# First unit of a decoder block without the shift of 256 features, its share added to the sums as a bias

## The chip, the core and the metric

The kernel runs on one core of one Trainium2 chip. A core has a matrix engine (TensorE, PE in the profile, with PEld for its weight loads), a vector engine (VectorE, DVE), an activation engine (ScalarE, ACT), a general engine (GpSimd, POOL) and a queue engine (SyncE, SP) that here issues every DMA. Each engine takes its instructions in order and waits on semaphores; the program fixes the order on each engine beforehand. The metric is the device time of one execution in microseconds (us); lower is better.

## The reference, cut to what matters

One layer, one sequence of 1024 tokens with 1024 features, all float32. The change touches only the first lines of the layer:

```python
mod = (cond @ w_ada[l] + b_ada[l])              # cond = silu(c), one vector of 1024
sh_a, sc_a, gt_a, sh_m, sc_m, gt_m = split(mod, 6)
h = rms_norm(x, g_attn_pre[l]) * (1 + sc_a) + sh_a
proj = h @ w_in[l]                              # 2304 columns: q, k, v of two mixers
...                                             # two attentions, w_out, gated residual
y = square(relu(h2 @ w_up[l])) @ w_down[l]      # the channel half, gated residual
```

Write `xn` for x divided by its root mean square. Then h = xn * g + s, with a scale g = g_attn_pre * (1 + sc_a) and a shift s = sh_a for each feature. A product with h is a product with xn * g, plus the row s @ w_in, which is the same for every token.

## The kernel before, in words

Every float32 product is done as three products of halves: each operand is split in a part rounded to the engine's fast type ("hi") and the rest ("lo"), and hi*hi, hi of the activations * lo of the weights (lines L920, L921) and lo of the activations * hi of the weights (L923) are added in one PSUM bank. `hw` holds hi and lo of h, transposed: feature chunk k (128 features, k = 0 to 7) by token.

The program is written out by a planner of the kernel's own (`Sched`), which runs when the program is built. Every piece of work is an operation with a booked duration, its dependences, the buffers it takes and gives (`Res`), and a priority; several operations may go to one of two engines, and the planner picks the one that ends earlier by its own figures. TensorE's work stands in streams ("xt" for transposes of x, "mod", "dense" for projections, "s", "t", "pv" for attention), and `prefer()` says which goes first: dense work is preferred as long as the projections lead the attention by less than `LEAD`, counted in units. What comes out is a fixed order on each engine.

**Loading.** SP issues, in the order of the list `order0`: the eight blocks of x (128 tokens each), the columns of `w_ada` for the shift and the scale of h (group g has the 256 features of chunks 2g and 2g+1; four tiles (g, j) of 512 KB, each with shift and scale columns side by side), and the six weight tiles of the first unit, ("w", i). `NWA` and `r_stg` are the buffers these go to, `WS` those of the raw weights, `WR` those of the split weights.

**Preparing.** For each block of x: ACT squares and sums it (L629), POOL adds epsilon and raises to -1/2 (L468, L470), ACT or DVE multiplies the block by that (L634, L635), TensorE transposes it in eight pieces (L642), ACT or DVE copies the result out of PSUM to `xnT` (L646). For each group: DVE multiplies eight 128x512 pieces of `w_ada` by `cond` and adds them up (L664, L666), TensorE sums over partitions (L675), and DVE makes g and s (L681 to L683). Then for each chunk: ACT writes hi (L705), ACT writes the full value in place (L702), DVE subtracts to get lo (L708). Group 0 does this in two halves of 512 tokens, the others at once.

**The first unit** (`first_unit`). A unit is a set of 384 columns of `w_in`: three column sets c by two token halves x, six PSUM banks, each summing eight chunks. There are six units. In the first, the six banks are filled side by side as the chunks become ready: chunks 0 and 1 for the first half, then for the second, then chunks 2 and 3 for both, 4 and 5, and at the end 6 and 7 bank by bank. While TensorE has nothing to do, `filler` puts in products of ones that nobody reads (L937) up to the first product of that bank. `evac` takes each finished bank out (on DVE the rotary embedding, L817 to L820; on ACT and DVE hi and lo). The next units use `proj_tile`: 24 products in a row in one of the two "pj" banks, after each other.

Attention, the output projection and the channel half follow. The code that is touched:

Of the kernel before, what the change touches and what calls it, by code (L numbers as in the profile page):

```python
# [177 lines left out]
class Sched:  # L178
# [57 lines left out]
    def spare(self, o):  # L236

        return self.slack if 15 <= o.prio < 25 else 2.5 if o.kind == "w" else 0.0
# [24 lines left out]
    def pick(self, e):  # L263
        best = None
        q = self.queue[e]
        for o in q:
# [9 lines left out]
            key = (s + PW * o.prio if e != "SP" else s, o.prio, o.seq)  # L276
# [81 lines left out]
def hybrid_block(ctx: ExitStack, tc: tile.TileContext, x, positions, w_ada, b_ada, g_attn_post, w_in, w_out,  # L358
# [33 lines left out]
    WR, WS, NP, NV, NK, NQ, NT, NO = 6, 2, 4, 3, 2, 2, 2, 2  # L392
# [89 lines left out]
    order0 = [("x", 0), ("x", 1), ("x", 2), (0, 0), (0, 1), ("x", 3), (0, 2), ("w", 0), (0, 3), ("w", 1)]  # L482
    order0 += [("x", t) for t in range(4, TB)]
    for g in range(1, 4):
        order0 += [(g, 0), (g, 1), (g, 2), (g, 3)] + [("w", 2), ("w", 3), ("w", 4), ("w", 5)][(0, 0, 1, 3)[g]:(0, 1, 3, 4)[g]]
# [30 lines left out]
    def load_ada(g, j):  # L516

        def emit():
            wa_t[g, j] = stage("wa") if (g, j) in beside else place0("wa")
            for n in range(2):  # L520
# [26 lines left out]
    def split_w(*a):  # L547
# [10 lines left out]
        if a[0] == 0:  # L558
            w_e[a] = op("DVE", t_dv(512), lo(V), [e], gives=[(r_wst, 1)], prio=3)
        else:  # L560
            w_e[a] = op(("DVE", "POOL"), (t_dv(512), t_ptt(512)), (lo(V), lo(G)), [e], gives=[(r_wst, 1)], prio=3)
# [21 lines left out]
    e = op("ACT", 0.1, lambda: A.activation(cond[:], c_raw, AF.Exp, scale=-1.0), [e_c], prio=0)  # L583
# [6 lines left out]
    warm = p0.tile([P, KC], F32, name="warm")  # L590
# [35 lines left out]
    def x_block(tb):  # L626
        def f_sq():
# [24 lines left out]

    def mod_group(g):

        b = {}
# [30 lines left out]
        for half in ((0, 1) if g == 0 else (None,)):  # L686
# [6 lines left out]
    def mod_chunk(k, eg, half):  # L693
# [6 lines left out]
        def full(eng):  # L700
            if eng is A:
                return lambda: A.activation(h, h, AF.Identity, bias=s_a[:, k:k + 1], scale=g_a[:, k:k + 1])  # L702
            return lambda: V.tensor_scalar(h, h, g_a[:, k:k + 1], s_a[:, k:k + 1], ALU.mult, ALU.add)

        eh = op("ACT", t_sb(n) + 2 * AP_COST, lambda: A.activation(hh, h, AF.Identity, bias=s_a[:, k:k + 1],  # L705
                                                                  scale=g_a[:, k:k + 1]), deps, prio=0)
        e = op("ACT", t_sb(n) + 2 * AP_COST, full(A), [eh], prio=0)
# [21 lines left out]
    e_turned = op("POOL", 1.8, f_turned, [e_rope] + e_rs, prio=0)  # L729
# [241 lines left out]
    for a in first_unit():  # L971
        evac(*a)
# [1270 lines left out]
```

## Time and profile before

| | before |
|---|---|
| time, median of 3 runs | 1117.04 us (1116.61 to 1117.36) |
| the profiled execution | 1117.15 us, its span 1114.9 us (2.25 us lie around the span) |
| granted clock of TensorE | 0.998 |
| TensorE busy | 1100.7 us, 5393 products |
| VectorE, ScalarE, GpSimd busy | 819.5, 630.3, 247.9 us |
| first product of the first unit (L920) | 23.16 us |
| the second half of chunk 0 begins | 34.70 us |
| first product of the second unit (`pj`, L920) | 66.87 us |

"Busy" of TensorE counts matmuls whose ends are modelled and overlap, so the distance from start to start is what to read, not the length. An order of start times on one engine is a timeline; a row with xN merges N equal instructions, and the brackets tell what ended an idle time before it. A view by windows adds up each engine's busy time in a stretch.

### The profile page before, as it was taken

The page shows a single profiled execution, that of the slowest core. Times are in us where ns is not written, and L with a number is a line of the kernel's source. Part 1 is how long each engine was busy: PE and PEld are TensorE (multiplying, and loading weights), DVE is VectorE, ACT ScalarE, POOL GpSimd, SP SyncE. Part 2 cuts the span into 40 slices and gives each one's busy share as a digit, 9 for nine tenths or more (in the row PEclk, how much of TensorE's full clock was granted, in tenths as well). Part 3 has the DMA queues.
Part 4 walks back from the last instruction along what each step waited for, and adds up shares of the span by engine and source line. Part 5 has one row for each costly group of instructions (what it writes and reads, how often), then busy time and mean ns, then how long its engine had stood idle before and what let it go on. Part 6 is the DMA issues. An engine that isn't in the chain of part 4 may idle for free.

```text
span 1114.9 us, 15568 instructions
## 1 busy us (share of the span) xinstructions
PE 1100.7 (99%) x5393; PEld 917.0 (82%) x5393; DVE 819.5 (74%) x1388; ACT 630.3 (57%) x1092; POOL 247.9 (22%) x316
## 2 busy tenths in 40 slices
PE   8999999999999999999999999999999999999996
PEld 7788888888888888888888888888888888888885
DVE  7877777666777666689798654798643996537998
ACT  8768776464656666577674335643154632347542
POOL 2158768666742231110000000000000000000003
PEclk9999999999999999999999999999999999999999
DMA  9756676454513734656751369521578013584104
GB/s 350 227 180 192 195 261 198 146 207 159 186 43 140 263 103 131 227 211 243 276 217 38 109 240 334 175 76 39 201 267 308 26 57 113 189 320 152 39 20 151
DMA packets 94110, 195.39 MB, mean 175 GB/s; under 512 B 9008, under 2 KB 31664, under 8 KB 94032
## 3 DMA queue, kind: packets, MB, share of 16 engines
q1 hardware_dynamic: 94032, 194.40, 50.3%
q8 instruction: 43, 0.70, 0.3%
q14 instruction: 35, 0.29, 0.1%
HBM read 141.80 MB, written 33.03 MB: 157 GB/s over the span
## 4 chain that ended last, share of the span: by engine, by line
PE 85%; DVE 7%; DMA 3%; issue 2%; ACT 1%; SPq 0%; POOL 0%; POOLq 0%; DVEq 0%; ACTq 0%
PE mlp_ps L2057 17%; PE mlp_ps L2055 17%; PE mlp_ps L2056 17%; PE pj L920 5%; PE pj L923 5%; PE pj L921 4%; PE s_ps L1203 3%; PE y_ps L1609 2%; PE y_ps L1611 2%; PE y_ps L1610 2%; PE o_ps L1338 2%; DMA wa<-in_w_ada 2%; PE pt_ps L1308 1%; PE s_ps L1258 1%; PE o_ps L1350 1%
## 5 line engine op out<-in xcount | busy, mean ns | idle before, releaser
L2055 PE MATMUL mlp_ps<-hw 128*128 128x512 f32 x896 | 348.9, 389 | 0.2 <-DVE u L2092 0.2
L2057 PE MATMUL mlp_ps<-hw 128*128 128x512 f32 x896 | 348.6, 389 | 0.0
L2056 PE MATMUL mlp_ps<-hw 128*128 128x512 f32 x896 | 348.6, 389 | 0.0
L2055 PEld LDWEIGHTS mlp_ps<-hw 128*128 128x128 f32 x896 | 168.2, 188 | 35.5 <-DVE u L2092 0.6
L2056 PEld LDWEIGHTS mlp_ps<-hw 128*128 128x128 f32 x896 | 168.2, 188 | 35.1
L2057 PEld LDWEIGHTS mlp_ps<-hw 128*128 128x128 f32 x896 | 168.2, 188 | 34.7
L1819 DVE TENSOR_TENSOR hw<-w,hw 128x1024 fp32r<-128x1024 f32 x96 | 114.6, 1221 | 98.1 <-ACT hw L1812 97.9
L1812 ACT CAST hw<-w 128x1024 fp32r<-128x1024 f32 x96 | 97.7, 1048 | 127.5 <-PE mlp_ps L2057 86.8
L2165 POOL TENSOR_TENSOR st<-st,nhalf 128x1 f32<-128x1 f32 x8 | 8.0, 1010 | 591.8 <-DVE st L2163 591.8
L920 PE MATMUL pj<-hw,w_hl 128*128 128x512 f32 x240 | 102.3, 426 | 0.0
L923 PE MATMUL pj<-hw,w_hl 128*128 128x512 f32 x240 | 94.6, 394 | 0.0
L921 PE MATMUL pj<-hw,w_hl 128*128 128x512 f32 x240 | 94.3, 393 | 0.0
L1326 DVE TENSOR_TENSOR ph<-pt_ps,ph 128x512 fp32r<-128x512 f32 (+1 forms) x110 | 69.1, 647 | 31.4 <-ACT ph L1322 31.0
L1812 ACT CAST hw<-u 128x1024 fp32r<-128x1024 f32 x48 | 48.6, 1051 | 63.2 <-PE mlp_ps L2057 63.2
L1322 ACT CAST ph<-pt_ps 128x512 fp32r<-128x512 f32 (+1 forms) x110 | 58.4, 556 | 31.5 <-PE pt_ps L1311 25.2
L1819 DVE TENSOR_TENSOR hw<-u,hw 128x1024 fp32r<-128x1024 f32 x48 | 56.9, 1218 | 17.8 <-ACT hw L1812 17.8
L1229 ACT ACTIVATE p_sb<-p_sb,mn 128x128 f32<-128x128 f32 (+3 forms) x64 | 49.7, 777 | 33.6 <-DVE mn L1222 32.9
L1234 POOL TENSOR_SCALAR p_sb<-p_sb,den 128x128 f32<-128x128 f32 (+3 forms) x64 | 49.8, 783 | 75.6 <-DVE den L1232 69.6
L2113 DVE TENSOR_TENSOR yacc<-yacc,mlp_ps 128x512 f32<-128x512 f32 x96 | 62.0, 681 | 3.3 <-PE mlp_ps L2057 3.3
L1070 POOL TENSOR_TENSOR ada_acc<-ada_acc,wa_st 128x512 f32<-128x512 f32 x42 | 55.6, 1323 | 3.5
L923 PEld LDWEIGHTS pj<-hw,w_hl 128*128 128x128 f32 x240 | 45.1, 188 | 10.4
L1609 PE MATMUL y_ps<-hw,oh 128*128 128x512 f32 x128 | 52.1, 407 | 0.0
(215 smaller groups left out, 1971.0 us busy)
## 6 DMA issues: line engine op xcount, KB each, us to landing
hw<-s_dram SPq DMA_DIRECT2D x84, 512.0 KB, 4.3
wa_st<-in_w_ada SPq DMA_DIRECT2D x32, 512.0 KB, 5.2
w<-in_w_up SPq DMA_DIRECT2D x32, 512.0 KB, 5.6
w<-in_w_down SPq DMA_DIRECT2D x32, 512.0 KB, 6.7
s_dram<-hw SPq DMA_DIRECT2D x28, 512.0 KB, 3.8
qt<-hl SPq DMA_DIRECT2D x40, 256.0 KB, 2.6
w_st<-in_w_in SPq DMA_DIRECT2D x36, 256.0 KB, 3.0
x_sb<-in_x SPq DMA_DIRECT2D x16, 512.0 KB, 5.5
```

The costliest lines, as they stand in the source:

```text
L920: T.matmul(ps, w[:, 0, n], h[0], start=(k == 0), stop=False)
L921: T.matmul(ps, w[:, 1, n], h[0], start=False, stop=False)
L923: T.matmul(ps, w[:, 0, n], h[1], start=False, stop=(k == KC - 1))
L1322: A.copy(b["ph"][:, 0, :w], b["pt"][:, :w])
L1326: V.tensor_tensor(b["ph"][:, 1, :w], b["pt"][:, :w], b["ph"][:, 0, :w].bitcast(F32), ALU.subtract)
L1609: T.matmul(ps[:], b["oh"][:, k], wh[:, c0:c0 + 512], start=(k == 4 * m), stop=False)
L1812: A.copy(out[j][0], flat(src[j]))
L1819: V.tensor_tensor(out[j][1], flat(src[j]), out[j][0].bitcast(F32), ALU.subtract)
L2055: T.matmul(ps[m][:], sh, mh, start=starts and k == 0, stop=False, **kw)
L2056: T.matmul(ps[m][:], sh, ml_, start=False, stop=False, **kw)
L2057: T.matmul(ps[m][:], sl, mh, start=False, stop=k == 3, **kw)
L2113: e = op("DVE", t_dv(512), lambda: V.tensor_tensor(y(), y(), ps[m][:], ALU.add), [e, ml.e_y[tb, n]], gives=gives, prio=1)
```

## The change

The numbers of lines below are of the changed kernel where they are above L978 or so named.

- **Group 0** (`LATE = (0,)`): its four tiles of `w_ada` are cut the other way: two tiles hold scale columns alone, two hold shift columns alone. The two with the scale are loaded early, the two with the shift (named (10, 0), (10, 1)) last of all. `late_sums` sums either, with 128x256 pieces.
- **Chunks 0 and 1** of h are first made without the shift: ACT writes hi of xn*g, and one DVE instruction (`scalar_tensor_tensor`) writes lo from xnT, g and hi. The full value is not written.
- **The bias**: once s of these 256 features is there, twelve small products (`pb`, 128x2) multiply it with the first unit's weights, DVE adds hi and lo, and ACT adds the outcome to each of the six finished banks (`shift`) before `evac`. The weight tiles 0 to 2 stay until then.
- **Again**: after that, `mod_chunk(..., again=True)` makes chunks 0 and 1 with the shift (ACT hi, DVE full value, DVE lo, 1024 tokens at once) for the units that follow; their products wait for `e_rest`.
- **GpSimd** multiplies all eight blocks of x by their norm, and five of the full values of chunks 2 to 7 go to it.
- **Order and tables**: `order0` is another list; three buffers for raw weights instead of two; priorities weigh 0.03 us each in the first unit; weight loads are held back 1.5 us instead of 2.5; no filler stands by itself in front of a product of the first unit; `LEAD` is 1.0 instead of 0.8; the activation table for Exp is loaded by an instruction that waits for no DMA.

```diff
-        return self.slack if 15 <= o.prio < 25 else 2.5 if o.kind == "w" else 0.0
+        return self.slack if 15 <= o.prio < 25 else 1.5 if o.kind == "w" else 0.0
...
-    WR, WS, NP, NV, NK, NQ, NT, NO = 6, 2, 4, 3, 2, 2, 2, 2
+    WR, WS, NP, NV, NK, NQ, NT, NO = 6, 3, 4, 3, 2, 2, 2, 2
...
+    LATE = (0,)
+    order0 = [('x', 0), ('x', 1), ('x', 2), ('w', 0), ('x', 3), (0, 0), (0, 1), ('w', 1), ('x', 4), ('x', 5), (1, 0), ('x', 6), ('x', 7), (1, 1), (1, 2), ('w', 2), (1, 3), (2, 0), (2, 1), (2, 2), (2, 3), ('w', 3), (3, 0), ('w', 4), (3, 1), ('w', 5), (3, 2), (3, 3), (10, 0), (10, 1)]
...
-        e = op(("ACT", "DVE"), (t_sb(D) + AP_COST, t_d2(D) + AP_DV),
-               (lambda: A.mul(x_t[tb][:], x_t[tb][:], rstd[:, tb:tb + 1]),
-                lambda: V.tensor_scalar(x_t[tb][:], x_t[tb][:], rstd[:, tb:tb + 1], None, ALU.mult)), [e], prio=2)
+        e = op("POOL", t_pts(D),
+               lambda: G.tensor_scalar(x_t[tb][:], x_t[tb][:], rstd[:, tb:tb + 1], 1.0, ALU.mult, ALU.mult), [e], prio=1)
...
+        if k // 2 in LATE and not again:
+            eh = op("ACT", t_sb(n) + AP_COST, lambda: A.mul(hh, h, g_a[:, k:k + 1]), deps, prio=0)
+            e = op("DVE", t_dv(n) + AP_DV, lambda: V.scalar_tensor_tensor(
+                hl, h, g_a[:, k:k + 1], hh.bitcast(F32), ALU.mult, ALU.subtract), [eh], prio=0)
...
+        if again:
+            eh = op("ACT", t_sb(n) + 2 * AP_COST, lambda: A.activation(hh, h, AF.Identity, bias=s_a[:, k:k + 1],
+                                                                      scale=g_a[:, k:k + 1]), [eg] + e_used[k], prio=6)
+            e = op(("ACT", "DVE"), (t_sb(n) + 2 * AP_COST, t_d2(n) + 2 * AP_DV), (full(A), full(V)), [eh], prio=4)
+            e_rest[k] = op("DVE", t_dv(n), lambda: V.tensor_tensor(hl, h, hh.bitcast(F32), ALU.subtract), [e], prio=4)
+            return
...
-        e = op("ACT", t_sb(n) + 2 * AP_COST, full(A), [eh], prio=0)
+        e = op(("ACT", "POOL"), (t_sb(n) + 2 * AP_COST, t_pts(n) + 0.6), (full(A), full(G)), [eh], prio=0)
...
-        n = int(max(0.75 * idle, 0.5 * min(o.dur, 2.0)) / 0.22)
+        n = int(max(0.75 * idle, 0.0 if o.dur in (0.454, 0.227) else 0.5 * min(o.dur, 2.0)) / 0.22)
...
+                if LATE:
+                    def shift(a=a, c=c):
+                        A.activation(accs[a][:], accs[a][:], AF.Identity, bias=bias0[:, c:c + 1])
+                    d = op("ACT", t_ps(512) + AP_COST, shift, [d, e_bias], prio=2)
...
+            for c in range(3):
+                for k, part in jobs:
+                    i, n = w_at(0, c, k)
+                    T.matmul(b_ps[0][:, c], w_hl[0, i][:, part, n * P:n * P + P], s_hl[:, k],
+                             start=(k, part) == jobs[0], stop=(k, part) == jobs[-1])
...
-    LEAD = 0.8
+    LEAD = 1.0
```

How the instructions stand is shown at three places. The first is TensorE from the fourth block of x (`pxt` are its transposes, `pm` the sums of group 0, `acc<-ones_r` filler, `acc<-hw,w_hl` the first unit). Before:

```order
L642 MATMUL pxt<-head,x_sb 128x128 x8
L937 MATMUL acc<-ones_r 128x512 x3
L675 MATMUL pm<-ones,acc_a 128x1 x4
L937 MATMUL acc<-ones_r 128x512 x6
L642 MATMUL pxt<-head,x_sb 128x128 x8
L937 MATMUL acc<-ones_r 128x512
L920 MATMUL acc<-hw,w_hl 128x512
L921 MATMUL acc<-hw,w_hl 128x512
L937 MATMUL acc<-ones_r 128x512
```

and with the change:

```order
L644 MATMUL pxt<-head,x_sb 128x128 x8
L995 MATMUL acc<-ones_r 128x512
L673 MATMUL pm<-ones,acc_a 128x1 x2
L995 MATMUL acc<-ones_r 128x512 x7
L978 MATMUL acc<-hw,w_hl 128x512
L979 MATMUL acc<-hw,w_hl 128x512
L644 MATMUL pxt<-head,x_sb 128x128 x8
L978 MATMUL acc<-hw,w_hl 128x512
L979 MATMUL acc<-hw,w_hl 128x512
```

The transposes of the fifth block have moved behind the first product, two of four sums of group 0 are gone from here, and filler no longer stands between the products.

The second place is GpSimd, from its first instruction on x (`rs_t`, `rstd` are the two steps of the norm). With the change:

```order
L468 TENSOR_SCALAR rs_t<-ssq 128x1
L470 TENSOR_TENSOR rstd<-rs_t,nhalf 128x1
L637 TENSOR_SCALAR x_sb<-x_sb,rstd 128x1024
L468 TENSOR_SCALAR rs_t<-ssq 128x1
L470 TENSOR_TENSOR rstd<-rs_t,nhalf 128x1
L468 TENSOR_SCALAR rs_t<-ssq 128x1
L637 TENSOR_SCALAR x_sb<-x_sb,rstd 128x1024
L470 TENSOR_TENSOR rstd<-rs_t,nhalf 128x1
L637 TENSOR_SCALAR x_sb<-x_sb,rstd 128x1024
```

Before, the pairs L468, L470 follow each other with no scaling between them. The rows are of the second, third and fourth block: the scaling of the third stands behind the first step of the fourth.

The third place is GpSimd behind its last step on x, up to the low parts of weights that the second unit needs (`turned`, `tab` are the tables of the rotary embedding, `w_hl` the split weights, `hl` the first bank's result). Before:

```order
L725 COPY turned<-cosw 128x8x8 x2
L726 COPY turned<-sinw 128x8x16
L728 TENSOR_SCALAR turned<-turned 128x8x16 x2
L733 COPY tab_150<-head 128x1024
L734 MEMSET tab_151 128x1024
L555 TENSOR_TENSOR w_hl<-w_st,w_hl 128x512 x2
L826 TENSOR_TENSOR hl<-hl 128x512
L555 TENSOR_TENSOR w_hl<-w_st,w_hl 128x512 x2
L1249 COPY p_sb<-nsink 128x4 x2
```

and with the change:

```order
L783 COPY turned<-cosw 128x8x8 x2
L784 COPY turned<-sinw 128x8x16
L786 TENSOR_SCALAR turned<-turned 128x8x16 x2
L791 COPY tab_150<-head 128x1024
L792 MEMSET tab_151 128x1024
L748 TENSOR_SCALAR xnT<-xnT,g_a,s_a 128x1024 x2
L557 TENSOR_TENSOR w_hl<-w_st,w_hl 128x512 x2
L748 TENSOR_SCALAR xnT<-xnT,g_a,s_a 128x1024 x3
L557 TENSOR_TENSOR w_hl<-w_st,w_hl 128x512 x4
L884 TENSOR_TENSOR hl<-hl 128x512 x2
L557 TENSOR_TENSOR w_hl<-w_st,w_hl 128x512
```

Five full values (L748) are new, two behind the tables and three behind two weight tiles; and six weight tiles (L557) stand ahead of the first bank's low part (L884, L826 before) instead of two.

On TensorE the products after the first unit are the same in number; from the 2633rd before the end on they also stand in the same order, in the middle of the attention they are woven in another way. `pb` adds twelve, and there are 45 fillers instead of 61.

More of the change, by code (lines that the diff above doesn't have):

```diff
@@ L558, in split_w @@
         if a[0] == 0:
-            w_e[a] = op("DVE", t_dv(512), lo(V), [e], gives=[(r_wst, 1)], prio=3)
+            w_e[a] = op(("DVE", "POOL"), (t_dv(512), t_ptt(512) + 1.5), (lo(V), lo(G)), [e], gives=[(r_wst, 1)], prio=3)
         else:
@@ L582, in hybrid_block @@
     e_init = op("DVE", 0.4, f_init, prio=0)
-    e = op("ACT", 0.1, lambda: A.activation(cond[:], c_raw, AF.Exp, scale=-1.0), [e_c], prio=0)
+    warm = p0.tile([P, KC], F32, name="warm")
+    e = op("ACT", 1.5, lambda: A.activation(warm[:], nhalf[:], AF.Exp), [e_init], prio=0)
+    e = op("ACT", 0.1, lambda: A.activation(cond[:], c_raw, AF.Exp, scale=-1.0), [e_c, e], prio=0)
     def f_cond():
@@ L964, in after @@
                     sc.filler = None
+                if last[w] == i:
+                    w_used(w)
             d = dense(0.454 if part == 0 else 0.227, emit,
                       [w_e[0, w_at(0, c, k)[0]], (e_hl if part else e_hh)[k, x]] + (e_xn[0] + e_xn[1] if a == 5 else []),
-                      takes=[(r, 1)] if first else [], after=after, gives=[(r_w, 1)] if last[w_at(0, c, k)[0]] == i else [])
+                      takes=[(r, 1)] if first else [], after=after)
+            if c == 2 and part:
+                e_used.setdefault(k, []).append(d)
```

101 lines of the change are left out of this document (87 added, 14 removed).

## The prediction

> **What bounds the kernel now.** I read the page first, then TensorE's waits from 66 us on, then its order in time over the start, then VectorE's and GpSimd's.
>
> ```profile
> PE 1100.7 (99%) x5393; PEld 917.0 (82%) x5393; DVE 819.5 (74%) x1388; ACT 630.3 (57%) x1092; POOL 247.9 (22%) x316
> ...
> PE pm_o L1581 <- DVE o_sb L1575: 0.4, 1, 0.4
> ```
>
> TensorE is busy for 99% of the span, and from 66 us to the end it waits five times, 0.4 us at the most; the longest is shown. So whatever moves its work before 66 us moves the end by as much, unless a new wait appears later. The start:
>
> ```profile
> 23.16 0.39 PE L920 MATMUL acc<-hw,w_hl 128*128 128x512 f32 x1
> ...
> 34.70 0.39 PE L920 MATMUL acc<-hw,w_hl 128*128 128x512 f32 x1
> ...
> 42.62 0.95 PE L675 MATMUL pm<-ones,acc_a 128*128 128x1 f32 x8
> 43.44 0.47 PE L920 MATMUL acc<-hw,w_hl 128*128 128x512 f32 x1
> 43.75 0.39 PE L921 MATMUL acc<-hw,w_hl 128*128 128x512 f32 x1
> ...
> 46.28 2.88 PE L923 MATMUL acc<-hw,w_hl 128*128 128x512 f32 x12
> 49.01 0.39 PE L920 MATMUL acc<-hw,w_hl 128*128 128x512 f32 x1
> ...
> 65.91 0.46 PE L891 MATMUL pv<-head,vt 64*128 64x64 f32 x4
> ...
> 66.87 0.39 PE L920 MATMUL pj<-hw,w_hl 128*128 128x512 f32 x1
> ...
> 24.00:56.00 32.00, 31.20 (x163) 25.35 (x162) 28.93 (x49) 25.49 (x34) 6.60 (x11) 1.00 0.78 246
> ```
>
> The first product starts at 23.16, the second half of chunk 0 at 34.70, the second unit (`pj`) at 66.87. A product takes (49.01 - 46.28) / 12 = 0.2275 us, eight small ones (`pm`, and so the eight transposes of a block) 0.82; the first product behind them takes 0.31, so a switch costs 0.08. The last row is a window: between 24 and 56 us TensorE is busy for 31.20 of 32 us, VectorE (third number) for 28.93, ScalarE for 25.49, GpSimd for 6.60. So VectorE has hardly more room than TensorE just where the change gives GpSimd new work. I forecast the start of `pj` and carry the difference to the end.
>
> **What VectorE and GpSimd do to each other.** This decides the forecast.
>
> ```profile
> 30.21 0.69 DVE L646 COPY xnT<-pxt 128x512 f32<-128x512 f32 x1
> 30.82 1.54 DVE L666 SCALAR_TENSOR_TENSOR acc_a<-wa,cond,acc_a 128x512 f32<-128x512 f32 x1
> ...
> 33.07 0.48 DVE L664 TENSOR_SCALAR acc_a<-wa,cond 128x512 f32<-128x512 f32 x1
> 33.59 0.75 DVE L666 SCALAR_TENSOR_TENSOR acc_a<-wa,cond,acc_a 128x512 f32<-128x512 f32 x1
> 34.25 0.68 DVE L555 TENSOR_TENSOR w_hl<-w_st,w_hl 128x512 fp32r<-128x512 f32 x1
> ...
> 76.08 0.70 DVE L819 TENSOR_TENSOR pj<-pj,tab 128x512 f32<-128x512 f32 x1
> ...
> 311.37 1.75 DVE L555 TENSOR_TENSOR w_hl<-w_st,w_hl 128x512 fp32r<-128x512 f32 x1 [0.23 <-ACT w_hl L550]
> ...
> 406.92 1.26 DVE L1664 SCALAR_TENSOR_TENSOR y_sb<-y_sb,st,gate_a 128x1024 f32<-128x1024 f32 x1
> ```
>
> ```profile
> 6.66 0.23 POOL L468 TENSOR_SCALAR rs_t<-ssq 128x1 f32<-128x1 f32 x1 [6.23 <-ACT junk L629]
> 6.97 0.57 POOL L470 TENSOR_TENSOR rstd<-rs_t,nhalf 128x1 f32<-128x1 f32 x1
> ...
> 25.79 0.73 POOL L468 TENSOR_SCALAR rs_t<-ssq 128x1 f32<-128x1 f32 x1 [3.13 <-ACT junk L629]
> 26.61 1.05 POOL L470 TENSOR_TENSOR rstd<-rs_t,nhalf 128x1 f32<-128x1 f32 x1
> ...
> 30.79 1.03 POOL L733 COPY tab<-head 128x1024 f32<-128x1024 f32 x1
> 31.77 0.95 POOL L734 MEMSET tab<- 128x1024 f32 x1
> ...
> 75.47 1.29 POOL L555 TENSOR_TENSOR w_hl<-w_st,w_hl 128x512 fp32r<-128x512 f32 x1 [5.25 <-ACT w_hl L550]
> ...
> 311.28 1.29 POOL L1070 TENSOR_TENSOR ada_acc<-ada_acc,wa_st 128x512 f32<-128x512 f32 x1
> ...
> 230.59 1.56 POOL L1234 TENSOR_SCALAR p_sb<-p_sb,den 128x1024 f32<-128x1024 f32 x1
> ...
> 407.18 1.89 POOL L1234 TENSOR_SCALAR p_sb<-p_sb,den 128x896 f32<-128x896 f32 x1 [2.72 <-PE pm_o L1581]
> ...
> L1234 POOL TENSOR_SCALAR p_sb<-p_sb,den 128x1024 f32<-128x1024 f32 x8 | 9.5, 1183 | 8.1 <-DVE den L1232 6.9 <-PE pt_ps L1308 1.2
> ```
>
> An accumulation (L666) takes 0.75 us; the one at 30.82, begun behind GpSimd's copy of 30.79, takes 1.54. A low part (L555) takes 0.68; that of 311.37, behind GpSimd's of 311.28, takes 1.75. So GpSimd held VectorE for 0.79 of its 1.03 us and for 1.06 of its 1.29: its own time less 0.24. The other way too: GpSimd's two steps of the norm take 0.73 and 1.05 beside accumulations and 0.23 and 0.57 without, and a scaling of 896 that starts in VectorE's L1664 lasts until 1.89. Whichever starts first keeps the other out, even where GpSimd reads a single operand (copy, scaling). Two things escape: VectorE work that reads PSUM (L819 keeps 0.70 beside GpSimd's row of 75.47), and the MEMSET, which reads nothing (31.77: the accumulation it overlaps ended at 32.36, as if the copy alone had held it).
>
> The Trainium skill (SBUF — State Buffer, section SBUF: two separate sides) states this as an exclusive lock: a VectorE instruction with two SBUF inputs, or in a 2-port mode, and a GpSimd instruction that reads SBUF have one port pair, and the first keeps it "for the whole instruction". By it each hold would be GpSimd's full time, 16.3 us in the sum below where the rows give 13.0: an estimate of 1127.0. The trace agrees with the lock, and shows 0.24 less for each.
>
> **The first product.** x is scaled on GpSimd with the form of L1234: eight take 9.5 us, one of them 1.56 and the rest 1.13 on average. I take 1.13; the low bound is the copy's 1.03, the high one 1.89, where VectorE is in the way. A hold is then 0.89. ScalarE is relieved of four scalings and now does squares, copies and hi only:
>
> ```profile
> 13.71 1.06 ACT L629 ACTIVATE junk<-x_sb 128x1024 bf16<-128x1024 f32 x1
> ...
> 18.05 1.08 ACT L646 COPY xnT<-pxt 128x512 f32<-128x512 f32 x2 [0.24 <-PE pxt L642]
> ...
> 21.27 1.50 ACT L705 ACTIVATE hw<-xnT,s_a,g_a 128x512 fp32r<-128x512 f32 x2
> 22.68 1.51 ACT L702 ACTIVATE xnT<-xnT,s_a,g_a 128x512 f32<-128x512 f32 x2
> ```
>
> With 2.5 MB instead of 3.3 loaded up to the fourth block, its square, at 13.71 before, comes 1 to 2 us sooner; its scaling, behind that and the third's, ends at 16.1 if nothing is held, and TensorE's transposes at 17.0. ScalarE then has two copies and a cast (1.08 for two), two squares (1.06 and read-out, 1.2) and hi of 0.7, so the first product would come at 20.4 to 21. The other input is the scale: on VectorE eight pieces of half width, by 16.7 unheld. GpSimd's second scaling falls on the steps ahead of `cond`, the fourth between the pieces (0.89 each), and the third's and fourth's small steps alternate with the pieces (0.9): 19.4. Sums and g take 1.2, hi 0.7 more: **first product 21.4, g ready at 20.6.**
>
> **From g to the second unit.** First TensorE alone: 144 products (32.8 us) from 20.4, the transposes of four blocks and of the tables (0.9 each with its switch: 4.5), sums of three groups and a half set for the shift (3.2), `pb` 1.4 (twelve tiny products at a `pm` record's 0.10, or at a product's 0.23: 1.3 to 2.7): 62.3, with some waiting 62.9. Now VectorE, whose order has the rotary embedding of the first bank ahead of `pj`:
>
> ```profile
> 36.31 1.29 DVE L708 TENSOR_TENSOR hw<-xnT,hw 128x512 fp32r<-128x512 f32 x2
> ...
> 37.70 0.16 DVE L682 TENSOR_TENSOR g_a<-g_a,head 128x2 f32<-128x2 f32 x1
> ...
> 39.81 2.20 DVE L666 SCALAR_TENSOR_TENSOR acc_a<-wa,cond,acc_a 128x512 f32<-128x512 f32 x3
> 41.93 2.35 DVE L708 TENSOR_TENSOR hw<-xnT,hw 128x1024 fp32r<-128x1024 f32 x2
> ...
> 67.84 0.42 DVE L902 TENSOR_TENSOR v_hl<-pv,v_hl 128x256 fp32r<-128x256 f32 x1
> ```
>
> Behind g stand 21 accumulations (2.20 / 3 = 0.735: 15.4 us), three first pieces (0.52 to the next: 1.6), four lo of 512 (0.65: 2.6), three weight lo and two copies (0.6: 3.0), eight lo of 1024 (1.135: 9.1; two of them are the values made again), eight pieces of 256 for the late shift (0.4, between the 0.42 of a subtraction and 0.735: 3.2), the small steps for g, s and bias (16 of some 0.14: 2.2), two full values (0.65: 1.3) and the embedding (four, 0.7: 2.8): 41.2 us. Unheld, g would be there at 17.9, and with 2.9 us of waits for transposes and values the embedding would end at **62.0**: TensorE at 62.9 would just be the later, and the change would bring 4 us.
>
> But GpSimd works beside it: the scalings of blocks 5 to 8 (4 times 0.89), the table's copy (0.79), five full values (5 times 0.89) and four lo of the second unit's weights (4 times 1.06): 13.0 us of holds. VectorE has no idle time to take them; nearly all its work there has two SBUF inputs. A hold costs nothing where VectorE waits or reads PSUM: two copies, sums for g and s, three quarters of the embedding; I take off two of the fourteen, 1.9. So 20.6 + 41.2 + 0.7 of waits + 13.0 - 1.9 = **73.6 for the embedding and `pj`, 6.7 us later than 66.87.** Bounds: with four more covered 70.0; if a value that GpSimd finishes late makes VectorE wait for it too (the lo behind it), 0.5 for each of five, 76.1. TensorE has gaps instead, where the sums of groups 1, 2 and the shift are late.
>
> The other edits lie beside this. The bias on ScalarE (six passes over 512, at most hi's 0.75 each) is hidden by the values made again on VectorE; with that cover gone the first pass would delay the embedding, and `pj`, by 0.75. The late shift is loaded last, but VectorE takes it behind all accumulations. Sixteen fillers fewer (0.2275 each) and two full values off ScalarE (22.68, 1.5) are inside the numbers above. Third raw buffer, `LEAD`, priorities: no price, they are in the order.
>
> By the order one `pv` more lies behind `pj` (four records, 0.4) and TensorE switches to dense work eight times less (8 times 0.08): -0.2 together. On the profiled execution 1117.15 + 6.7 - 0.2 = 1123.7; its median stands 0.1 lower. **1123.6.**
>
> **Rivals.**
>
> *GpSimd finds the gaps.* No hold reaches `pj`: TensorE is the bound at 62.9, `pj` 4.0 earlier, 1113.4 with 0.3 for ties. It decides if under 0.9 us of the 13.0 stay on VectorE's path; with up to 4.9 it is still no loss. For it: between 24 and 56 us GpSimd was busy 6.60 us before, and only one accumulation shows a long hold. Against: most of those 6.60 were steps on 128x1, small copies and the MEMSET; the one large reading instruction held. 15%.
>
> *Only copies and two-input work hold* (0.79 + 4 times 1.06 = 5.0), scalings don't: 62.0 + 5.0 - 0.5 covered = 66.5, 1116.8. For it: no row shows a scaling that holds VectorE from its first moment. Against: 407.18, where VectorE kept a scaling out, so it wants the same thing. 10%.
>
> *The attention adds to it.* ScalarE's hi of the second half's bank c=1 now waits, for a buffer, for three GpSimd steps on `w_ada` (the last of the form of 311.28, 1.29) which stand behind weight lo that are themselves held; three times 1.29, 3.9 us, on the way to the first exponentials, past what the projections cover: 1127.5. 8%.
>
> **How the numbers follow.** The forecast has 67%, its own range 1120.0 to 1126.2. A difference under 0.2% (2.2 us) can't be told from no change. Slower by more: forecast and third rival, less a little, 0.74; within: second rival, 0.10; faster: the first and the second's edge, 0.16. For eight in ten: 1115.0 to 1128.0, leaving out the first rival and a worse third.
>
> **What would show it.** Right: accumulations and lo of 1.5 to 1.8 us on VectorE wherever a scaling, value or weight lo of GpSimd starts just before, some twelve of them from 20 to 70 us; GpSimd's small steps at 0.7 to 1.1; TensorE waiting for VectorE between 30 and 70; `pj` near 73.6. Wrong: those rows at 0.75 and 0.68 and `pj` near 63; or `pj` as forecast with another end, which would put the rest in the attention.

## The result, and the profile after

The changed kernel takes **1131.81 us** (median of 4 runs, 1130.92 to 1137.14), the kernel before beside it 1117.2 (1116.61 to 1117.45). By these medians it is slower by 14.6 us; the ratio is **1.0141 [1.011, 1.0173]**. Ratios, here and below, are taken over all fast runs and not from the medians, and two executions of over 3000 us (one of the kernel before, one with the MEMSETs below) are left out. 1123.6 was forecast, 6.4 above the kernel before, with a range up to 1128.0: the sign was right, the size less than half, and the time lies outside the range. The profiled execution took 1131.57 us; its span is 1129.0 against 1114.9 before, 14.1 more.

The page of the changed kernel, first part, then the waits of TensorE up to 110 us (in total, times, longest):

```profile
PE 1106.2 (98%) x5389; PEld 920.8 (82%) x5389; DVE 836.1 (74%) x1402; ACT 626.5 (55%) x1097; POOL 267.5 (24%) x318
```

```profile
PE pm L673 <- DVE acc_a L666: 3.2, 1, 3.2
PE pxt L644 <- POOL x_sb L637: 2.6, 5, 0.8
PE ptab L802 <- POOL turned L786: 1.9, 1, 1.9
```

TensorE is still busy for 98%, but it now waits where it did not before, for VectorE's accumulations and for GpSimd. Its order in time:

```profile
20.87 0.50 PE L978 MATMUL acc<-hw,w_hl 128*128 128x512 f32 x1
...
33.12 1.06 PE L802 MATMUL ptab<-head,turned 128*64 128x128 f32 x8 [1.92 <-POOL turned L786]
...
34.50 1.70 PE L718 MATMUL pm<-ones,acc_a 128*128 128x1 f32 x8
...
37.06 0.63 PE L978 MATMUL acc<-hw,w_hl 128*128 128x512 f32 x1
37.49 0.63 PE L979 MATMUL acc<-hw,w_hl 128*128 128x512 f32 x1
...
63.57 0.58 PE L673 MATMUL pm<-ones,acc_a 128*128 128x1 f32 x4 [3.21 <-DVE acc_a L666]
...
66.14 2.55 PE L1064 MATMUL pb<-s_hl,w_hl 128*128 128x2 f32 x12
...
77.30 0.39 PE L978 MATMUL pj<-hw,w_hl 128*128 128x512 f32 x1
```

The first product comes at 20.87 (before 23.16) and `pj` at 77.30 (before 66.87): 2.3 us were won and 12.7 lost between the two. From `pj` to the end it is 1129.0 - 77.30 = 1051.7 us, against 1048.0 before: another 3.7 lost there. And something that no row of before shows: behind both gaps TensorE itself is slower. A product took 0.2275 us; at 37 us the next one starts 0.43 later, eight `pm` take 1.70 instead of 0.95. The windows of the changed kernel (window, us, busy time of PE, PEld, DVE, ACT and POOL, then the granted TensorE clock, the share of the DMA engines, GB/s) show the same as clock:

```profile
30.00:40.00 10.00, 8.08 (x36) 6.72 (x35) 9.11 (x15) 6.67 (x10) 7.61 (x9) 0.72 1.09 357
40.00:50.00 10.00, 10.00 (x47) 8.20 (x46) 9.86 (x12) 1.77 (x3) 4.77 (x3) 0.94 0.67 177
...
60.00:70.00 10.00, 6.79 (x29) 5.73 (x28) 8.60 (x13) 5.30 (x7) 4.15 (x4) 0.76 0.19 53
70.00:80.00 10.00, 10.00 (x41) 8.20 (x40) 9.76 (x13) 7.54 (x15) 5.39 (x5) 0.90 0.42 145
```

Before, every such window from 20 to 1110 us has 1.00. Here 0.72 at 30 to 40 and 0.76 at 60 to 70 stand beside the two gaps.

VectorE's and GpSimd's order in the changed kernel:

```profile
36.58 4.81 DVE L709 SCALAR_TENSOR_TENSOR acc_a<-wa,cond,acc_a 128x512 f32<-128x512 f32 x4
41.32 2.31 DVE L766 TENSOR_TENSOR hw<-xnT,hw 128x1024 fp32r<-128x1024 f32 x1
...
55.94 1.52 DVE L666 SCALAR_TENSOR_TENSOR acc_a<-wa,cond,acc_a 128x256 f32<-128x256 f32 x3
...
58.85 4.58 DVE L666 SCALAR_TENSOR_TENSOR acc_a<-wa,cond,acc_a 128x256 f32<-128x256 f32 x4
...
68.73 0.16 DVE L1074 COPY bias<-pb 128x3 f32<-128x3 f32 x1 [1.23 <-PE pb L1064]
...
75.33 0.69 DVE L878 TENSOR_TENSOR hl<-hl,acc 128x512 f32<-128x512 f32 x1
```

```profile
38.06 2.80 POOL L748 TENSOR_SCALAR xnT<-xnT,g_a,s_a 128x1024 f32<-128x1024 f32 x2 [2.39 <-ACT hw L763]
40.83 3.94 POOL L557 TENSOR_TENSOR w_hl<-w_st,w_hl 128x512 fp32r<-128x512 f32 x2
...
59.19 2.57 POOL L748 TENSOR_SCALAR xnT<-xnT,g_a,s_a 128x1024 f32<-128x1024 f32 x2 [6.79 <-ACT hw L763]
```

Four accumulations at 36.58 take 4.81 us beside GpSimd's two full values of 38.06; at 0.735 each they would take 2.94. A lo at 41.32 takes 2.31 beside the weight lo of 40.83, where before two took 2.35. Four pieces of half width at 58.85 take 4.58 beside two values and the weight lo behind them (61.72); three unheld ones at 55.94 take 1.52. The embedding ends at 75.33 + 0.69 = 76.0 us. TensorE does not wait for it here: from 64.01 to 77.30 it works without a gap, from 65.2 to 72 at half speed, and `pj` comes when they are done. The wait for VectorE that counts in this execution is the 3.21 us ahead of the late sums. The groups by shape between 20 and 76 us give the sum, first before, then after (busy, mean ns of one):

```profile
L666 DVE SCALAR_TENSOR_TENSOR acc_a<-wa,cond,acc_a 128x512 f32<-128x512 f32 x21 | 16.5, 788 | 0.5
```

```profile
L709 DVE SCALAR_TENSOR_TENSOR acc_a<-wa,cond,acc_a 128x512 f32<-128x512 f32 x21 | 21.3, 1012 | 0.5
```

The same 21 accumulations cost 4.8 us more. Over all of VectorE's instructions in that stretch, one by one against the unheld duration of the same form, 13 are held, for 11.0 us together (before: one, 0.8): three beside scalings, one beside the copy of the table, five beside full values, four beside weight lo.

### The profile page after: what moved, and what is told of

Same layout as the page of the kernel before. It is cut to its first block, busy times and chain, and to the rows that moved or that the text cites. A ratio compares the mean times of both kernels' runs of the same rounds, so it can differ in the third digit from the quotient of the medians.

```text
span 1129.0 us, 15575 instructions
## 1 busy us (share of the span) xinstructions
PE 1106.2 (98%) x5389; PEld 920.8 (82%) x5389; DVE 836.1 (74%) x1402; ACT 626.5 (55%) x1097; POOL 267.5 (24%) x318
## 4 chain that ended last, share of the span: by engine, by line
PE 77%; DVE 12%; issue 4%; DMA 2%; ACT 2%; POOL 2%; SPq 1%; POOLq 0%; DVEq 0%; ACTq 0%
PE mlp_ps L2165 16%; PE mlp_ps L2167 16%; PE mlp_ps L2166 16%; PE pj L978 4%; PE pj L981 3%; PE pj L979 3%; PE s_ps L1313 3%; PE y_ps L1719 1%; PE y_ps L1720 1%; PE y_ps L1721 1%; PE o_ps L1448 1%; PE s_ps L1368 1%; PE pt_ps L1418 1%; PE pt_ps L1425 1%; PE o_ps L1460 1%
## 5 line engine op out<-in xcount | busy, mean ns | idle before, releaser
L978 PE MATMUL pj<-hw,w_hl 128*128 128x512 f32 x240 | 102.0, 425 | 0.0
L1344 POOL TENSOR_SCALAR p_sb<-p_sb,den 128x128 f32<-128x128 f32 (+3 forms) x64 | 52.1, 819 | 84.8 <-DVE den L1342 63.0
```

Source lines behind the costliest of these rows:

```text
L978: T.matmul(ps, w[:, 0, n], h[0], start=(k == 0), stop=False)
```

## The experiments

The theory: GpSimd's new instructions that read SBUF hold VectorE. The rivals: that GpSimd's work is harmless (the order, the late shift or the settings cost the time), and, from the trace after, that TensorE's clock is a cost of its own. Each ratio is to the kernel before, timed beside it on the same chip. Starts of `pj` and spans behind it are read from one execution of each kernel. They are less certain than the medians: with the MEMSETs below `pj` starts 2 us later than in the kernel before and the time is the same, and two executions of the changed kernel take 1051.7 and 1053.5 us from `pj` to the end.

### GpSimd's new work without reading: both parts, and one

The same program in the same order; GpSimd writes a constant where it multiplied. First the eight scalings and the five values, then the values alone (the second hunk).

```diff
-               lambda: G.tensor_scalar(x_t[tb][:], x_t[tb][:], rstd[:, tb:tb + 1], 1.0, ALU.mult, ALU.mult), [e], prio=1)
+        e = op("POOL", t_pts(D), lambda: G.memset(x_t[tb][:], 1.0), [e], prio=1)
...
+            if eng is G:
+                return lambda: G.memset(h, 1.0)
```

> The changed kernel, its order untouched on every engine, but GpSimd's eight scalings of x and its five full values are MEMSETs of 1.0 into the same tiles: they write as much, read nothing and take about the same time (0.95 instead of 1.13 us); x is left unscaled and five values are wrong, so nothing else about the work changes. Theory 1 (VectorE and GpSimd shut each other out): the four scalings behind the first product and the five values stop holding VectorE, 9 x 0.9 = 8 us, and the first product comes 1 us earlier; the embedding of the first bank ends near 67 instead of 76.05, the first product of the second unit starts near 67.5 instead of 77.30, 1131.8 becomes 1121 to 1123. Theory 2 (the loss is the late shift itself: more work on VectorE, two chunks made twice, bias): nothing on VectorE is saved, within 2 us of 1131.8. Theory 3 (TensorE's clock, which fell to half behind two gaps): it follows the gaps, so with theory 1 products between 36 and 41 and between 65 and 71 are back at 0.2275 us; if the clock were the cause and the holds not, gaps and clock stay.

> As the kernel before this one in the list, but only the five full values on GpSimd are MEMSETs; x is scaled as in the changed kernel. Theory 1: five holds of 0.9 go, 4.5 us, and with them the 3.2 us gap of TensorE ahead of the sums of the late shift and the half clock behind it: the second unit starts near 71, 1126. Theory 2: 1131.8.

Both constant: 1121.44 us, 1.0039 [1.0025, 1.0053], `pj` at 68.81. Values alone: 1126.16, 1.0084 [1.0059, 1.0108], `pj` at 71.32. So the values' reading is worth 5.7 us, the scalings' 4.7 (x also comes sooner: the first product is at 19.83), and 4.1 are left. What is held on VectorE between 20 and 76 us falls from 11.0 to 5.7 without the values' reading, and to 3.7 without both. The rival that instructions of this form, with one operand in SBUF, hold nothing falls with this.

### The lock by itself, in the kernel before

Behind the copy and the MEMSET of the table, eight copies of 128x1024 into a buffer that nobody reads; and eight MEMSETs of the same size instead.

```diff
+            junk = p0.tile([P, D], F32, name="junk2", tag="junk2", bufs=1)
+            for _ in range(8):
+                G.tensor_copy(junk[:], scl[0].to_broadcast([P, D]))
...
+                G.memset(junk[:], 0.0)
```

> The kernel before with the disputed cost alone: eight more copies on GpSimd (128x1024, the form of the table's copy, into a tile that nobody reads) right behind the table's MEMSET, at 32.7 to 42 us, where GpSimd had nothing to do until 57.5; the order on all other engines is the old one. Theory 1: each holds VectorE's accumulations and lo for 0.79, 6.3 us; 2.5 to 4 of them go into VectorE's two waits at 53 and 58, so the second unit starts 3 to 6 us later, with half clock behind TensorE's gaps: 1121 to 1125. Rival (GpSimd finds gaps): 1117.4 within 1.

> As the kernel before this one in the list, with eight MEMSETs (128x1024, near 0.95 us each, reading nothing) in place of the eight copies. Theory 1: VectorE is not held, 1117.4 within 1. If it is GpSimd's writing, or its being busy, that holds VectorE: as the copies.

The copies: 1124.26 us, 1.0061 [1.0046, 1.0076]. The MEMSETs: 1118.01, 1.0002 [0.9992, 1.0012]. GpSimd, VectorE and TensorE with the copies, in time:

```profile
33.22 11.22 POOL L743 COPY junk<-head 128x1024 f32<-128x1024 f32 x8
```

```profile
36.26 1.52 DVE L555 TENSOR_TENSOR w_hl<-w_st,w_hl 128x512 fp32r<-128x512 f32 x1
37.70 2.96 DVE L666 SCALAR_TENSOR_TENSOR acc_a<-wa,cond,acc_a 128x512 f32<-128x512 f32 x2
40.58 2.96 DVE L708 TENSOR_TENSOR hw<-xnT,hw 128x512 fp32r<-128x512 f32 x2
...
43.65 0.80 DVE L682 TENSOR_TENSOR g_a<-g_a,head 128x2 f32<-128x2 f32 x1
```

```profile
42.16 1.65 PE L929 MATMUL acc<-hw,w_hl 128*128 128x512 f32 x3 [4.94 <-DVE hw L708]
```

and with the MEMSETs:

```profile
33.71 8.36 POOL L743 MEMSET junk<- 128x1024 f32 x8
```

```profile
34.12 0.82 DVE L664 TENSOR_SCALAR acc_a<-wa,cond 128x512 f32<-128x512 f32 x1
...
35.64 0.69 DVE L555 TENSOR_TENSOR w_hl<-w_st,w_hl 128x512 fp32r<-128x512 f32 x1
36.24 1.53 DVE L666 SCALAR_TENSOR_TENSOR acc_a<-wa,cond,acc_a 128x512 f32<-128x512 f32 x2
37.70 1.28 DVE L708 TENSOR_TENSOR hw<-xnT,hw 128x512 fp32r<-128x512 f32 x2
```

Eight VectorE instructions are held beside the eight copies, 6.0 us together. TensorE then waits 4.94 us for a lo among them, and its clock falls too (three products in 1.65 us at 42.16), so the 6.8 us of the whole are not the lock alone. Beside the MEMSETs no instruction with two inputs is held. What holds those is GpSimd's reading, not its work. Even 128x2 elements wait (0.80 instead of 0.16). An instruction with one input is another matter: the TENSOR_SCALAR at 34.12 takes 0.82 instead of 0.48 beside the MEMSETs, and in the kernel with both parts constant and fillers (below) one at 18.54 takes 1.31 beside a MEMSET begun at 18.62. So a MEMSET did hold VectorE there.

### The two engines' work given back, and one part alone

Three kernels, each planned again by the kernel's own order rules. The scaling and the values back on ScalarE and VectorE, the late shift kept; the scaling on GpSimd in the kernel before; and no late shift, with GpSimd's work kept.

```diff
-        e = op("POOL", t_pts(D),
+        e = op(("ACT", "DVE"), (t_sb(D) + AP_COST, t_d2(D) + AP_DV),
...
-        e = op(("ACT", "POOL"), (t_sb(n) + 2 * AP_COST, t_pts(n) + 0.6), (full(A), full(G)), [eh], prio=0)
+        e = op("ACT", t_sb(n) + 2 * AP_COST, full(A), [eh], prio=0)
```

> The changed kernel with GpSimd's two new jobs taken back: x is scaled by ScalarE or VectorE as before, full values are on ScalarE as before; late shift, order of loads, buffers, filler rule and LEAD stay. The order on the engines is planned anew. Theory 1: VectorE has only the low parts of weights on GpSimd beside it, 4 holds; it ends its chain near 67 and the second unit starts near 68: 1118 to 1120, that is still 1 to 3 us over before, since VectorE has 4 us of work more there than before (chunks made again, lo of two chunks with a scale). Theory 2: 1130. If the late shift were a gain by itself: 1113 to 1115.

```diff
-        e = op(("ACT", "DVE"), (t_sb(D) + AP_COST, t_d2(D) + AP_DV),
+        e = op("POOL", t_pts(D),
```

> The kernel before with one part of the change alone: GpSimd scales the eight blocks of x; order of loads, shift, values stay; the order on the engines is planned anew. Theory 1 (each GpSimd instruction that reads SBUF keeps VectorE out): 5 or 6 of the 8 scalings fall where VectorE is busy, 0.9 each, 4.5 to 5.4 us; VectorE waited 2.45 us for ScalarE ahead of the last two lo and 1.55 ahead of the embedding, so 1 to 4 us reach the second unit, which starts near 68 to 71 instead of 66.87: 1118 to 1121. Rival: ScalarE, freed of four scalings, brings the first product forward and TensorE is the bound: 1115 to 1116.

```diff
-    LATE = (0,)
+    LATE = ()
```

> The changed kernel without the late shift (LATE empty, the four tiles of group 0 loaded together behind the fourth block of x); GpSimd's scalings and values, order list, buffers, filler rule and LEAD stay; planned anew. From the first product of the second unit to the end the kernel before takes 1048.0 us, the changed one 1051.7, the one with MEMSETs and fillers 1053.0. If the late shift (bias passes, chunks made again, first keys late) makes that part longer, it is 1048 to 1049 here; if LEAD, buffers and priorities do, 1051 to 1053. The second unit itself: VectorE has 4 us of work less, GpSimd two values more (2 holds): 73 to 76, so 1124 to 1130 in all.

The first took 1129.39 us, 1.0106 [1.0091, 1.0121]: nine more than the upper end expected, a miss. TensorE's order and a window show where it begins:

```profile
17.98 1.06 PE L645 MATMUL pxt<-head,x_sb 128*128 128x128 f32 x8 [2.55 <-DVE x_sb L638]
...
23.86 0.63 PE L979 MATMUL acc<-hw,w_hl 128*128 128x512 f32 x1
```

```profile
20.00:30.00 10.00, 10.00 (x39) 8.20 (x40) 8.13 (x14) 6.25 (x11) 6.67 (x13) 0.68 1.10 352
```

The scaling on VectorE makes the fourth block late, TensorE waits 2.55 us, and its clock is 0.68 in ten microseconds in which it doesn't wait at all. The second took 1127.56, 1.0086 [1.0071, 1.0101], 6.6 more than the upper end of what was expected: gaps of 1.69, 1.63 and 2.36 us, a clock of 0.83 at 40 to 50. The third, in whose list of loads the four tiles of group 0 stand together again, took 1131.42, 1.0129 [1.0114, 1.0144]; 1124 to 1130 was expected. That is the same as with the late shift (1131.81): in the presence of GpSimd's work the late shift costs and brings nothing.

### The clock

The kernel before without its 61 fillers; the changed kernel with fillers ahead of the transposes of the table (8) and of the late sums (14); the same with fillers also ahead of the sums of groups 2 (12) and 3 (3); and the changed kernel once more beside them.

```diff
-        n = int(max(0.75 * idle, 0.5 * min(o.dur, 2.0)) / 0.22)
+        n = 0
```

> The kernel before without its 61 filler products (they are read by nobody), all else planned as it was. Theory 3 (TensorE's clock falls behind gaps and stays low for some 6 us of work): the granted clock is near 0.5 to 0.7 from 10 to 40 us, where TensorE has many gaps, and the first unit's products take 0.425 us until the clock is back; 30 products at +0.2 and the transposes: the second unit starts 3 to 6 us later, 1120 to 1123. If the clock does not follow TensorE's gaps: the second unit up to 2 us earlier, 1115.

```diff
+            for _ in range(0 if i else 14):
+                T.matmul(b["all"][:], ones_r[:, :P], ones_r[:], start=True, stop=True)
...
+                for _ in range(0 if x else 8):
+                    T.matmul(b_tab[x][:].rearrange("p j t -> p (j t)"), ones_r[:, :P], ones_r[:], start=True, stop=True)
```

> The changed kernel plus 22 filler products that nobody reads: 8 ahead of the transposes of the tables (TensorE waited 1.9 us there) and 14 ahead of the sums of the late shift (3.2 us). Nothing else is touched. Theory 3 (behind each gap the granted clock falls, 0.72 and 0.76 in those ten microseconds, and products take 0.425 instead of 0.2275 us): with the gaps filled the twelve tiny products take 1.4 instead of 2.55 us, VectorE waits 1.2 us less for them, the products behind run at full speed, the second unit starts near 74.5 instead of 77.30: 1129. Theory 1 alone (only VectorE sets that moment): the clock is of no matter, 1131.8 within 0.7.

```diff
+            for _ in range({2: 12, 3: 3}.get(g, 0)):
+                T.matmul(b["all"][:], ones_r[:, :P], ones_r[:], start=True, stop=True)
```

> The changed kernel with fillers ahead of every place where TensorE waited over 1.5 us in one of its executions: 8 ahead of the tables' transposes, 12 and 3 ahead of the sums of groups 2 and 3, 14 ahead of the late shift's. In the run with two of these places filled the gap and the half clock came back at 42.6 us, and the embedding still ended at 76.5. Theory 3: with none left the granted clock is 1.00 from 12 to 80 us, sums and pb take their short time, VectorE waits 2 us less for them, the second unit starts near 74.5: 1129, and the times agree better with each other. If the holds alone set it: 1130 to 1132.

> The changed kernel once more, to stand beside the others on the same chip: 1130.9 to 1132.1 as before, all theories.

Without fillers the kernel before takes 1127.18 us, 1.0083 [1.0067, 1.01], four more than the upper end expected: a gap of 5.36 us at 38.4 and a clock of 0.66 behind it. With the first two groups of fillers the changed kernel takes 1130.28, 1.0111 [1.0094, 1.0128], only half of the gain expected, because the gap came back at the sums of group 2:

```profile
45.65 0.56 PE L721 MATMUL pm<-ones,acc_a 128*128 128x1 f32 x2 [3.07 <-DVE acc_a L712]
```

With all of them it takes **1128.18**, 1.0091 [1.0076, 1.0106] (the changed kernel again: 1132.06, 1.0124 [1.0104, 1.0143]). Its windows, and the first product of the second unit:

```profile
30.00:40.00 10.00, 9.96 (x53) 8.06 (x52) 9.79 (x14) 6.88 (x11) 7.21 (x8) 1.00 1.09 357
...
60.00:70.00 10.00, 10.00 (x54) 8.49 (x53) 9.83 (x14) 6.58 (x10) 4.08 (x4) 1.00 0.20 61
```

```profile
74.63 0.47 PE L986 MATMUL pj<-hw,w_hl 128*128 128x512 f32 x1 [0.72 <-DVE hl L886]
```

The clock is 1.00 throughout, VectorE is as full as before (held for 11.4 us), the embedding ends at 74.5 and `pj` starts at 74.63. With the clock kept, `pj` does wait for the embedding. So the clock is worth about 4 us, of which 77.30 - 74.63 = 2.7 show at `pj`; 0.6 of these are a sooner start of this execution (g ready at 19.42 instead of 20.06, ahead of every added filler). It also makes the time uncertain: four runs with fillers lie within 1.2 us, four of the changed kernel within 6.2, and the longest (1137.14) has the lowest mean clock (0.987, against 0.994 for the shortest).

### What is left: the part behind `pj`

Three more: constants as above and 13 fillers, so that neither hold nor clock is new; the same with `LEAD` at 0.8, the value before; and the changed kernel with `LEAD` at 0.8.

```diff
-    LEAD = 1.0
+    LEAD = 0.8
```

> MEMSETs for GpSimd's scalings and values (x and five values wrong, order kept) and fillers in the gaps that were left then: 2 ahead of the tables, 8 ahead of the sums of group 2, 3 ahead of the late shift's. Holds and half clock both gone but for the weights' lo: the second unit starts near 67.5, and with the 3.7 us that the part behind it takes longer 1119 to 1120, that is 1.5 to 2.5 us over before. If holds and clock were all of the loss: 1117 or less.

> The kernel with MEMSETs for GpSimd's scalings and values and fillers in the gaps (1121.3), with LEAD back at 0.8: the second unit starts at 66.8 as there. If LEAD 1.0 costs the part behind it 2 us or more: 1118 to 1119. If not: 1121.3 within 0.7.

> The changed kernel with LEAD back at 0.8. Up to the second unit nothing changes (77.3). From there to the end the changed kernel took 3.7 us more than the one before (1051.7 against 1048.0). If LEAD weaves the attention so that TensorE waits (0.8 and 0.5 us ahead of o_ps), 2 us of it go: 1130. If the loss comes from what the first unit leaves behind (the first keys late, one pv more, waits of 0.9 for the first scores), no difference: 1131.8 within 0.7.

And the settings alone (no late shift, no work for GpSimd: the order of loads, the buffers, priorities, hold-back of weights, filler rule and `LEAD` remain):

```diff
-    LATE = (0,)
+    LATE = ()
...
-        e = op("POOL", t_pts(D),
+        e = op(("ACT", "DVE"), (t_sb(D) + AP_COST, t_d2(D) + AP_DV),
...
-        e = op(("ACT", "POOL"), (t_sb(n) + 2 * AP_COST, t_pts(n) + 0.6), (full(A), full(G)), [eh], prio=0)
+        e = op("ACT", t_sb(n) + 2 * AP_COST, full(A), [eh], prio=0)
```

> Neither late shift nor new work on GpSimd: what is left of the change is the list of loads, three buffers for raw weights, priorities of 0.03 in the first unit, weight loads held back 1.5 us, the filler rule, LEAD 1.0 and the early table load. The second part (second unit to end): 1048 to 1049 if the late shift was its cost, 1051 to 1053 if these settings are. The first part: no holds but the old ones; gaps without filler bring half clock, 69 to 73. In all 1119 to 1125; if these settings alone are a gain: under 1117.

Constants with fillers: 1121.28 us, 1.003 [1.0018, 1.0042]. `pj` starts at 66.77, 0.1 before the kernel before, and yet the span is 1119.8: from `pj` to the end it is 1053.0, 5 more than before. The time is 1.3 us over what was expected. With `LEAD` 0.8 it takes 1122.67, 1.0049 [1.0034, 1.0064], and 1055.9 behind `pj` (in the longest of its four runs; two take 1121.4 and 1121.5); the changed kernel with 0.8 takes 1132.72, 1.0129 [1.0106, 1.0153]. So `LEAD` is not what costs. The settings alone take 1123.31, 1.0055 [1.0038, 1.0072]: `pj` at 69.72 and 1051.7 behind it. TensorE's waits behind 80 us in that kernel:

```profile
PE o_ps L1461 <- DVE ph L1437: 1.1, 1, 1.1
PE s_ps L1314 <- DVE mn L1333: 1.0, 2, 0.7
```

The longer part behind `pj` is there without the late shift and without GpSimd's work. But it is not the settings alone either: with the old settings it takes 1049.5 us with the eight copies, 1050.0 without fillers and 1051.0 with the scaling on GpSimd, where `pj` comes 7.6 to 9.3 us late, against 1048.0. Whether the settings (the list, the third buffer, priorities, the hold-back of 1.5 us) or the mere delay of `pj` make these waits was not taken apart, and stays open.

No version is faster than the kernel before. The medians make one chain: before 1117.4, settings 1123.3 (+5.9), GpSimd's work added 1131.4 (+8.1), late shift added 1131.8 (+0.4). The shares depend on the order: with the late shift added to the settings first it is 1129.4 (+6.1), and GpSimd's work on top costs 2.4. The planner makes a new order each time, and the gaps and the clock that follow are part of each step.

## Why the prediction was right and wrong

**Right: the holds.** VectorE is late for TensorE because GpSimd's reading holds it. `pj` does wait for the embedding where the clock is kept (74.63, a wait of 0.72 us); in the changed kernel as it was timed, TensorE met VectorE's delay sooner, at the late sums, and reached `pj` 1.3 us after the embedding, with slow products in between. The size of the holds was right: 14 times 0.79 to 1.06 less 1.9 made 11.1 us, and 11.0 were measured, 11.4 with the clock kept. The Trainium skill (SBUF — State Buffer, section SBUF: two separate sides) gives the loser's wait as the whole instruction of the other. The trace agrees with who waits; in the size, the rows' 0.24 less was the better guide, since the sum came out at 11.0.

**Right: the first product**, 20.87 against 21.4.

**Right, and tested twice: the sum on VectorE.** With all holds and the full clock it gave 73.6 for the embedding; the run with fillers has 74.5. With copies and weight lo alone (the second rival's condition, made true by the constants) it gave 66.5 for `pj`; the run has 66.77. Part of both is luck. Counted from g, which was ready at 19.42 with the fillers and not at 20.6, the first is 2.1 us short: the piece of 256, put at 0.4 us "between" two rows, takes 0.5 (three take 1.52), some 0.7 for eight, and VectorE stood idle for 2.2 us where 0.7 were counted. In the second, g came at 18.62 and not at 17.9, and VectorE was idle for 1.9 us and not for 2.9.

**Wrong: that TensorE's speed is given.** The term "TensorE alone: 62.9" and every step with a gap counted products at 0.2275 us, because before has a clock of 1.00 in every window. The prediction did say that "TensorE has gaps instead", and gave them no price. They cost 2.0 to 2.7 us up to `pj`: two periods at 0.43 us a product, in which the sums and `pb` that VectorE waits for are slow too (1.23 us for `pb`; twelve take 2.55 us, where 1.4 was in the sum). The sixteen fillers taken out were counted as 0.2275 us each; the run without any shows that they are there to keep the clock.

**Wrong: "-0.2 together" behind `pj`.** It measured +3.7. TensorE waited 1.92 us there before and 4.83 after. That the order of the products is the same was taken for the same waits. A kernel with the settings alone has 3.7 more as well, kernels with the old settings and a late `pj` 1.5 to 3.0; the cause of these waits stays open.

The sum of the span: 6.5 as predicted, 1.0 too little for the embedding, 2.7 for the clock (0.6 of them the start), 3.9 behind `pj`: 14.1.

**The rivals.** "GpSimd finds the gaps" fell: 13 instructions are held. "Only copies and two-input work hold" fell: the reading of values and scalings is worth 5.7 and 4.7 us. "The attention adds to it" happened, in small. ScalarE's hi waits for GpSimd as described (first row), and TensorE's wait for the scores behind it is 0.9 us, not 3.9:

```profile
85.34 1.07 ACT L892 ACTIVATE hl<-acc 128x512 fp32r<-128x512 f32 x2 [2.99 <-POOL ada_acc L1180]
```

```profile
87.81 1.08 PE L1368 MATMUL s_ps<-kt,qt 128*128 128x128 f32 x8 [0.90 <-DMA qt<-hl]
```

## What to carry to other kernels

Before work is given to an idle GpSimd, ask whether VectorE is full in that stage: what GpSimd reads from SBUF is paid by VectorE almost in full (11 us of holds on 13 instructions here). What it only writes held no instruction with two inputs, but some with one. Where TensorE is the bound, a gap of two microseconds can cost more than itself, since the products behind it may run at half speed; price every new gap with that, and look at what fillers are for before removing them. An unchanged order of instructions in a later stage is no proof of unchanged waits there.

## What the runs showed of the hardware

**The clock falls after short gaps, with a delay, and not always.** In the changed kernel TensorE waits 1.92 us up to 33.12; products stay at full speed until 34.50 and are slow until about 41: some 6.8 us, in which each 0.2275 becomes 0.43. The same kernel, run again, shows the same gap and no fall, and a fall behind its next gap (at 45.41):

```profile
33.03 1.06 PE L802 MATMUL ptab<-head,turned 128*64 128x128 f32 x8 [1.92 <-POOL turned L786]
...
45.41 1.79 PE L718 MATMUL pm<-ones,acc_a 128*128 128x1 f32 x8 [2.20 <-DVE acc_a L709]
```

Windows cut where the clock changes show more, first of the changed kernel, then of the run again:

```profile
31.04:34.45 3.41, 1.49 (x11) 1.28 (x11) 3.37 (x5) 2.27 (x5) 3.41 (x5) 1.00 1.08 360
34.45:41.28 6.83, 6.83 (x21) 5.67 (x20) 5.98 (x9) 4.32 (x6) 4.44 (x5) 0.50 1.09 336
...
61.76:65.17 3.41, 1.60 (x9) 1.47 (x10) 3.31 (x7) 0.50 (x1) 1.39 (x1) 1.00 0.26 70
65.17:72.00 6.83, 6.83 (x24) 5.88 (x23) 5.54 (x8) 4.61 (x7) 2.36 (x1) 0.50 0.16 43
```

```profile
28.39:31.81 3.42, 2.10 (x13) 1.24 (x11) 3.35 (x5) 1.91 (x4) 3.42 (x5) 1.00 1.08 356
31.81:35.22 3.41, 2.19 (x19) 2.10 (x19) 3.38 (x5) 1.80 (x4) 3.41 (x4) 1.00 1.09 358
```

The falls at 34.45 and 65.17 and the returns at 41.28 and 72.00 lie 2, 7 and 2 steps of 3.413 us apart. In the run again the falls are at 45.46 and 65.94 and the first return at 52.28 (2 and 4 steps), so the grid of steps lies elsewhere in the program. That fits the one gap with two outcomes. In the first execution it lies within one step, in which TensorE is busy for 1.49 of 3.41 us, and the fall follows at the end of that step. In the second a border at 31.81 cuts it in two, with 2.10 and 2.19 us busy, and the clock stays. No sharp bound follows: in the changed kernel with `LEAD` 0.8 a fall at 89.98 stands behind a step with 2.15.

The Trainium skill (TensorE: Matmul & The Clock Gate, section What's actually happening) knows two speeds, 4/8 and 8/8, and puts the fall behind an idle window of about 3.4 us that runs free of the program. The halving agrees (0.43 against 0.2275), and so do the step of 3.41 us and the dependence on chance; gaps of 1.7 to 2.4 us were enough here, shorter than that window.

**The lock is blind to size.** In the kernel with the work given back, a copy of 128x2 on VectorE stands behind a weight lo of GpSimd and takes 1.25 us instead of 0.17:

```profile
62.07 1.25 DVE L1055 CAST s_hl<-s_a 128x2 fp32r<-128x2 f32 x1
```

GpSimd pays too: its eight copies took 1.40 us each beside a full VectorE; the copy of the table, which began ahead of VectorE's accumulation, took 1.03.
